# Two hybrid decoder layers on one core: the sparse indexer's heads paced by the projections instead of issued in bursts

## The chip, the cores and the metric

One core of a Trainium2 chip. The metric is the device time of one execution in microseconds (us). The kernel before takes 1270.34 us, the median of three runs (1268.72 to 1270.92). The engines are named as in the profile: PE multiplies matrices (PEld loads its weights), DVE, ACT and POOL do elementwise work, SP issues the transfers.

## The reference, cut to what matters

`x` is 512 tokens of 1024 features. It is normalized once, then goes through two layers of this form (rotary embedding is `rope`; layer 0 and layer 1 differ in weights alone):

```python
def hybrid_layer(x, p_i, positions, w_in, sinks, idx_k_g, idx_k_b, w_o, ...):
    qa, ka, va, qb, kb, vb, qi, ki, wi = split(x @ w_in)
    qi = rope(qi.reshape(B, S, IDX_HEADS, IDX_DIM), positions)
    ki = rope(layer_norm(ki, idx_k_g, idx_k_b), positions)
    wi = wi * (IDX_HEADS ** -0.5 * IDX_DIM ** -0.5)
    oa = swa_sink_attention(rope(qa), rope(ka), va, sinks)
    # inside dsa_sparse_attention, for each block of 128 queries:
    #   sc = einsum('bqhd,bsd->bqhs', qi, ki)
    #   idx_score = einsum('bqhs,bqh->bqs', relu(sc), wi), causal
    #   sel = the 128 best keys of each query; softmax attention over those
    ob = dsa_sparse_attention(rope(qb), rope(kb), vb, qi, ki, wi, k_top)
    x = layer_norm(DN_ALPHA * x + concat(oa, ob) @ w_o, ln1_g, ln1_b)
    g, u = split(x @ w_gu)
    ple = (p_i @ w_pp) * sigmoid(x @ w_pg)
    return layer_norm(DN_ALPHA * x + (silu(g) * u) @ w_down + ple, ln2_g, ln2_b)
```

There are 8 index heads of 32 features. The key `ki` of a token is shared by the heads and has a layer norm of its own with the gain `idx_k_g`.

## The kernel before, in words

The 512 tokens are four blocks t = 0 to 3 of 128. Every float32 product is made of three passes over a high and a low part (`mm3`, L317, L318, L319), so most of PE's instructions come from those three lines. `fh` and `fl` are the two parts of the residual stream with features in the partitions. `to_features` makes them: PE transposes (L430) a block into two PSUM banks, ACT copies the high part (L432), DVE subtracts for the low part (L433). PSUM has 8 banks in one rotation, all under the name `bank`.

**The front of a layer** is `start()`. For each block it projects the 296 index columns (256 of the queries, 32 of the key, 8 of the head weights), with `gi_out` behind the product. Then come the 384 key and value columns for two pairs of blocks (`kv_out`) and two of the four query projections of 256 columns (`q_out`). `gi_out` takes mean and variance of the index key from PSUM (L559, L560), copies the key into the tile `kin` (L558), and rotates the queries (`rope`: DVE L507, POOL L509, a rounded high part L512, the low part L513). For every second block it finishes the key's norm for two blocks: a reciprocal root in ten small DVE instructions (L349 to L356), then subtract the mean and multiply by the gain (L575), then multiply by the root and add (L576).

**Held turns.** What `gi_out` leaves must be transposed by PE (`turn`: PE L519, ACT L520). PE would have to wait for DVE and POOL if this came at once, so `order.later(delay, fn)` holds it: `Order` adds up an estimate of PE's time, and the held function runs when the sum has grown by `delay`. The index turns are held by D_GI = 9, the key turns by D_K = 8, the query turns by D_Q = 10.

**The index stream** is `index()`. For t = 1, 2, 3 it waits until the turns of its block are there. Then it writes one matmul for each of 8 heads over the keys up to its block (L650, 256, 384 or 512 columns), with ACT's relu behind it (L652) and DVE's weighted sum into `work` (L653). `topk()` follows on DVE: 16 steps of L664 and L665 for a block, then a mask (L667) which the sparse attention's scores read (L693).

**The order of the streams** is made by `Order.run`. Each stream is a generator with a clock of its own; the one furthest behind goes next, and what it yields is added to its clock. A stream that yields None waits, and its clock stands still. So `index()`, which has waited through the projections, has the lowest clock by far when its turns are there, and its heads come one after another until it has caught up. A scheduler behind this places each engine's instructions, and waits are added where one engine needs another.

**Before the first layer** the input norm of block 0 runs on DVE; blocks 1 to 3 take their sums on ACT (`ln_in_sums`: L374 the sum, L369 the squares), DVE applies them in `ln_in` (L389, L392). The rotary tables (`rotary`) are made on POOL and ACT beside that. `nsink`, the negated sinks, is one DVE instruction (L496). Weights arrive by SP, ACT rounds their high part (L270), POOL subtracts for the low part (L271).

## Time and profile before

| | |
|---|---|
| median of three runs | 1270.34 us (1268.72 to 1270.92) |
| the profiled execution | 1271.32 us, of it 1269.3 us span |
| mean granted clock of PE | 0.991 |
| PE busy | 1238.0 us, 98% of the span |
| DVE busy | 802.1 us, 63% |
| POOL busy | 702.3 us, 55% |
| ACT busy | 575.4 us, 45% |
| chain that ended last | PE 89%, DVE 4%, ACT 3%, POOL 2%, DMA 1% |

The span runs from the first to the last instruction; the profiled execution's own time has 2.0 us more around it. The clock is given in parts of 2.4 GHz: 1.00 is that level, 0.50 is 1.2 GHz. The chain is followed back from the last instruction: at each step to what released it. Its engine shares say whose work the end hung on. In the timelines the figure in brackets is idle time of the engine just before the row, with what ended it.

### The profile page before, as it was taken

The numbers are of one execution on the slowest core, as the hardware profiler recorded it, in microseconds if no ns is written. First come the engines' busy times: TensorE is split into PE (matmuls) and PEld (weight loads), VectorE is DVE, ScalarE is ACT, GpSimd is POOL, SyncE is SP. The second block draws the span as 40 slices with busy tenths as digits, with TensorE's granted clock in tenths as the row PEclk, the third lists the DMA queues.
The fourth block names the chain that finished last, engine by engine and source line by source line (L and its number), as shares of the span: only waits on it lengthen the run. The fifth ranks groups of instructions, "written<-read, shape, count | busy, mean of one in ns | idle before, by whom it ended". The sixth has DMA issues, their size and how long they took to land.

```text
span 1269.3 us, 18252 instructions
## 1 busy us (share of the span) xinstructions
PE 1238.0 (98%) x6632; PEld 1071.2 (84%) x6632; DVE 802.1 (63%) x1729; ACT 575.4 (45%) x1193; POOL 702.3 (55%) x579
## 2 busy tenths in 40 slices
PE   7899999999999999999999999999999999999996
PEld 5899989888888888888898998988888888888885
DVE  7889866764646363635679996675736364545376
ACT  6467764343333333434336677633434243433320
POOL 6687532367475756563067855233757574747422
PEclk9899999999999999999998999999999999999998
DMA  5133211333242424034023313114232323221321
GB/s 174 51 100 101 81 53 35 100 117 116 67 133 68 131 78 126 29 114 139 2 81 98 106 39 120 43 35 142 88 120 79 121 83 116 89 94 48 103 83 50
DMA packets 89123, 112.77 MB, mean 89 GB/s; under 512 B 5445, under 2 KB 65861, under 8 KB 89033
## 3 DMA queue, kind: packets, MB, share of 16 engines
q1 hardware_dynamic: 88360, 111.58, 28.2%
q8 instruction: 52, 0.85, 0.3%
q14 instruction: 39, 0.31, 0.1%
q10 hardware_dynamic: 672, 0.03, 0.0%
HBM read 109.49 MB, written 2.10 MB: 88 GB/s over the span
## 4 chain that ended last, share of the span: by engine, by line
PE 89%; DVE 4%; ACT 3%; POOL 2%; DMA 1%; issue 1%; DVEq 0%; ACTq 0%; SPq 0%; POOLq 0%
PE bank L317 26%; PE bank L318 26%; PE bank L319 26%; PE bank L689 3%; PE bank L731 2%; PE bank L725 2%; PE bank L519 1%; DMA wst<-in_w_pg_dram 1%; POOL wsp L271 1%; PE bank L430 1%; ACT wsp L270 1%; PE bank L748 1%; DVE x L413 1%; ACT bank L652 0%; DVE x L415 0%
## 5 line engine op out<-in xcount | busy, mean ns | idle before, releaser
L271 POOL TENSOR_TENSOR wsp<-wst,wsp 128x1024 fp32r<-128x1024 f32 (+2 forms) x148 | 351.5, 2388 | 270.9 <-ACT wsp L270 270.3
L318 PE MATMUL bank<-fl,wsp 128*128 128x512 f32 (+1 forms) x768 | 284.9, 372 | 0.4 <-DVE fl L433 0.4
L317 PE MATMUL bank<-fh,wsp 128*128 128x512 f32 (+1 forms) x768 | 283.6, 372 | 1.0 <-ACT fh L432 1.0
L319 PE MATMUL bank<-fh,wsp 128*128 128x512 f32 (+1 forms) x768 | 283.2, 371 | 0.0
L270 ACT CAST wsp<-wst 128x1024 fp32r<-128x1024 f32 (+2 forms) x148 | 151.4, 1032 | 166.4 <-PE bank L319 123.0
L881 DVE TENSOR_TENSOR t2k<-bank,t2k 128x512 f32<-128x512 f32 x44 | 30.4, 692 | 221.7 <-PE bank L319 221.7
L317 PE MATMUL bank<-wsp,fh 128*128 128x256 f32 (+3 forms) x512 | 166.9, 328 | 2.8 <-ACT fh L432 2.1
L319 PE MATMUL bank<-wsp,fl 128*128 128x256 f32 (+3 forms) x512 | 165.0, 325 | 1.8 <-DVE fl L433 1.1
L318 PEld LDWEIGHTS bank<-fl,wsp 128*128 128x128 f32 x768 | 144.7, 188 | 25.7 <-DVE fl L433 0.9
L317 PEld LDWEIGHTS bank<-fh,wsp 128*128 128x128 f32 x768 | 143.6, 188 | 26.7 <-ACT fh L432 1.9
L319 PEld LDWEIGHTS bank<-fh,wsp 128*128 128x128 f32 x768 | 144.7, 188 | 24.8
L318 PE MATMUL bank<-wsp,fh 128*128 128x256 f32 (+3 forms) x512 | 165.5, 324 | 0.0
L249 POOL TENSOR_TENSOR wsp<-slot,wsp 128x512 fp32r<-128x512 f32 x100 | 142.2, 1447 | 28.9 <-ACT wsp L248 28.9
L317 PE MATMUL bank<-wsp,slot 128*128 128x512 f32 x392 | 153.4, 391 | 0.0
L318 PE MATMUL bank<-wsp,slot 128*128 128x512 f32 x392 | 152.6, 389 | 0.0
L319 PE MATMUL bank<-wsp,slot 128*128 128x512 f32 x392 | 148.7, 390 | 0.0
L806 DVE TENSOR_TENSOR x<-bank,x 128x512 f32<-128x512 f32 x140 | 91.5, 684 | 88.5 <-PE bank L319 88.5
L911 ACT CAST slot<-t2k 128x256 fp32r<-128x256 f32 (+1 forms) x104 | 49.8, 497 | 144.0 <-DVE t2k L881 102.5
L249 POOL TENSOR_TENSOR wsp<-t2k,wsp 128x512 fp32r<-128x512 f32 x40 | 57.6, 1450 | 91.8 <-ACT wsp L248 91.8
L317 PEld LDWEIGHTS bank<-wsp,fh 128*128 128x128 f32 x512 | 98.7, 193 | 10.0 <-ACT fh L432 3.2
L319 PEld LDWEIGHTS bank<-wsp,fl 128*128 128x128 f32 x512 | 98.3, 193 | 7.7 <-DVE fl L433 1.6
L318 PEld LDWEIGHTS bank<-wsp,fh 128*128 128x128 f32 x512 | 98.9, 193 | 5.4
(169 smaller groups left out, 2174.0 us busy)
## 6 DMA issues: line engine op xcount, KB each, us to landing
wst<-in_w_gu_dram SPq DMA_DIRECT2D x88, 512.0 KB, 3.5
slot<-in_w_down_dram SPq DMA_DIRECT2D x80, 256.0 KB, 2.8
wst<-in_w_in_dram SPq DMA_DIRECT2D x16, 512.0 KB, 3.6
wst<-in_w_o_dram SPq DMA_DIRECT2D x16, 512.0 KB, 3.7
wst<-in_w_pg_dram SPq DMA_DIRECT2D x16, 512.0 KB, 4.1
wst<-in_w_in_dram SPq DMA_DIRECT2D x8, 256.0 KB, 2.8
lng<-in_ln_g_dram SPq DMA_DIRECT2D x4, 512.0 KB, 4.8
lnb<-in_ln_b_dram SPq DMA_DIRECT2D x4, 512.0 KB, 5.6
```

The costliest lines, as they stand in the source:

```text
L249: G.tensor_tensor(w[:, 1, j], src[j], w[:, 0, j], OP.subtract)
L270: A.copy(w[:, 0, :a * n], st[:, :a * n])
L271: G.tensor_tensor(w[:, 1, :a * n], st[:, :a * n], w[:, 0, :a * n], OP.subtract)
L317: PE.matmul(o, sh, mh, start=start, stop=False, skip_group_check=again)
L318: PE.matmul(o, sh, ml, start=False, stop=False, skip_group_check=again)
L319: PE.matmul(o, sl, mh, start=False, stop=stop, skip_group_check=again)
L689: PE.matmul(ps[:, o:o + nn], qT[kind, t, g][:, j * 128:(j + 1) * 128], kT[c, s][:, k0:k0 + nn], start=(s == 0), stop=(s == 1))
L725: PE.matmul(o, vt[b0 + b][:, f:f + 128], pts[b][:, u], start=b == 0 and u == 0, stop=b == nb - 1 and u == 1)
L731: PE.transpose(ps[:, j * 128:(j + 1) * 128], es[j][:, b * 128:(b + 1) * 128], idf)
L806: V.tensor_tensor(xt[t][:, c], ps, xt[t][:, c], OP.add)
L881: V.tensor_tensor(a, ps[1, f], a, OP.mult)
L911: A.copy(h[0], src)
```

## The change

Five edits, in the order of the diff.

1. `run` takes `credit=False`, used for `start()` with `index()`: a stream that waited begins again at the highest clock of the streams that did not wait. The index heads then come in turn with the projections.
2. The turns of the last block (t = 3, with the key of blocks 2 and 3) are held by D_KI = 13 instead of D_GI = 9. For blocks 0 to 2 the delay stays.
3. The copy into `kin` (L558) is gone. The subtraction of the mean and product with the gain stands right behind the block's mean and variance, and reads PSUM.
4. The sums of blocks 2 and 3 and the second half of the rotary tables are written inside `start()`, behind block 0's `to_features`; the sums of block 2 may not be placed ahead of ACT's second copy of the high part.
5. `nsink` is written at block 2, behind the last norm's DVE instruction.

```diff
--- before.py
+++ after.py
@@ -34,7 +34,7 @@
 THETA = 10000.0
 QA, KA, QB, KB, QI, NIN = 0, 512, 768, 1280, 1408, 1704
 NSLOT, NTMP = 28, 12
-D_GI, D_K, D_Q, AHEAD = 9.0, 8.0, 10.0, 2
+D_GI, D_KI, D_K, D_Q, AHEAD = 9.0, 13.0, 8.0, 10.0, 2
 IDX_PACE, NSTART, R_MAIN, R_TOP = 1.5, 2, 0.75, 0.001
 LAG, FILL = dict(a=1, b=2), {2: 6, 5: -2}
 QS = [("a", 0), ("a", 1), ("b", 0), ("b", 1)]
@@ -64,9 +64,12 @@
         while self.held:
             self.held.pop(0)[1]()
 
-    def run(self, *streams):
+    def run(self, *streams, credit=True):
+
+
 
         live = [[0.0, n, g, r] for n, (g, r) in enumerate(streams)]
+        waited = set()
         while live:
             live.sort(key=lambda e: e[:2])
             for e in live:
@@ -75,8 +78,13 @@
                 except StopIteration:
                     live.remove(e)
                     break
-                if c is not None:
+                if c is None:
+                    waited.add(e[1])
+                else:
                     c, pace = c if isinstance(c, tuple) else (c, c)
+                    if e[1] in waited and not credit:
+                        e[0] = max([e[0]] + [o[0] for o in live if o[1] not in waited])
+                    waited.discard(e[1])
                     e[0] += pace / e[3]
                     self.tick(c)
                     break
@@ -429,7 +437,7 @@
                 k = 4 * j + i
                 PE.transpose(ps[:, i * 128:(i + 1) * 128], xt[t][:, k * 128:(k + 1) * 128], idf)
             pv = ps.rearrange("p (a n) -> p a n", a=4)
-            A.copy(fh[:, 4 * j:4 * j + 4, ts], pv)
+            last["copy"] = A.copy(fh[:, 4 * j:4 * j + 4, ts], pv).ins
             V.tensor_tensor(fl[:, 4 * j:4 * j + 4, ts], pv, fh[:, 4 * j:4 * j + 4, ts], OP.subtract)
 
 
@@ -486,14 +494,10 @@
     ln_in(0)
     table = rotary()
     next(table)
-    for t in range(1, NT):
-        ln_in_sums(t)
-    for _ in table:
-        pass
+    ln_in_sums(1)
     bcast_row(ikg.rearrange("p a b -> p (a b)"), idx_k_g, 0, L * ID)
     bcast_row(ikb.rearrange("p a b -> p (a b)"), idx_k_b, 0, L * ID)
     bcast_row(sink.rearrange("p a b -> p (a b)"), attn_sinks, 0, L * NH)
-    V.tensor_scalar(nsink, sink, -1.0, None, op0=OP.mult)
 
     def rope(src, t, n, d, hi, lo, dup, each=False, top=None):
 
@@ -555,9 +559,10 @@
                 kin[t] = sm(2 * ID, "kin").rearrange("p (u d) -> p u d", u=2)
                 kmv[t] = sm(4, "kmv").rearrange("p (u d) -> p u d", u=2)
             st = sm(6, "kst6")
-            V.tensor_copy(kin[t - u][:, u], ps[:, 256:288])
             V.bn_stats(st, ps[:, 256:288])
             V.bn_aggr(kmv[t - u][:, u], st)
+            V.scalar_tensor_tensor(kin[t - u][:, u], ps[:, 256:288], kmv[t - u][:, u, 0:1], ikg[:, l],
+                                   op0=OP.subtract, op1=OP.mult)
             qs = []
             if t > 0:
                 wi[t] = small.tile([128, IH], F32, name="wi", tag="wi", bufs=4)
@@ -572,7 +577,6 @@
                 kn, mv = kin[t0], kmv[t0]
                 rs = rstd_of(mv[:, :, 1], 2)
                 for i in range(2):
-                    V.scalar_tensor_tensor(kn[:, i], kn[:, i], mv[:, i, 0:1], ikg[:, l], op0=OP.subtract, op1=OP.mult)
                     V.scalar_tensor_tensor(kn[:, i], kn[:, i], rs[:, i:i + 1], ikb[:, l], op0=OP.mult, op1=OP.add)
                 ks = slot()
                 iv = ks[:, :256].rearrange("p (t s u d) -> p t s u d", t=2, s=2, u=2)
@@ -587,7 +591,7 @@
                     turn(qiT[t, j], q, 4)
                 ready.add(("i", t))
                 order.tick(0.6)
-            order.later(D_GI, turns)
+            order.later(D_GI if t < NT - 1 else D_KI, turns)
 
         def kv_out(t, ps):
 
@@ -825,11 +829,20 @@
                 if l == 0 or t == 3:
                     to_features(t)
                     yield 0.9
+                if l == 0 and t == 0:
+                    with tc.issue_after(last["copy"]):
+                        ln_in_sums(2)
+                    ln_in_sums(3)
+                    for _ in table:
+                        pass
                 if l == 0 and t + 1 < NT:
                     ln_in(t + 1)
                 done = gi_out
                 if l == 0 and t + 1 < NT:
                     done = behind(last["norm"], gi_out)
+                if l == 0 and t == 2:
+                    with tc.issue_after(last["norm"]):
+                        V.tensor_scalar(nsink, sink, -1.0, None, op0=OP.mult)
                 yield from project(ws, 296, (t,), from_f, done, 3 * (t == 3))
             ws = take(4)
             for b in ALL:
@@ -847,7 +860,7 @@
                 for b in ALL:
                     yield from project(ws, 512, b, from_ma, res_out(h, ALPHA), 2 * (b is ALL[-1]))
 
-        order.run((start(), 1.0), (index(), 1.0))
+        order.run((start(), 1.0), (index(), 1.0), credit=False)
         load_gb(("1", l), ln1_g, ln1_b, l * D)
         order.run((rest(), R_MAIN), (attention(), 1.0), (topk(), R_TOP))
         order.flush()
```

Line numbers move by 4 to 8: `mm3` is L325, L326, L327, the turns L523, the index heads L654, L656, L657, POOL's weight parts L279, the low part of a rotation L517.

**PE, layer 0, at the index stream.** Before, all heads of t = 1, all turns of t = 2 and 3 and all heads of t = 2 stand between two groups of the 384-column projection (`x8`: eight in a row):

```order
L319 MATMUL bank<-wsp,fl 128x384
L650 MATMUL bank<-slot 128x256 x8
L519 MATMUL bank<-idr,slot 128x128 x18
L650 MATMUL bank<-slot 128x384 x8
L317 MATMUL bank<-wsp,fh 128x384
L318 MATMUL bank<-wsp,fh 128x384
```

With the change two heads of t = 1 stand there, then the turns of t = 2, then three heads, and the projection goes on:

```order
L327 MATMUL bank<-wsp,fl 128x384
L654 MATMUL bank<-slot 128x256 x2
L523 MATMUL bank<-idr,slot 128x128 x8
L654 MATMUL bank<-slot 128x256 x3
L325 MATMUL bank<-wsp,fh 128x384
L326 MATMUL bank<-wsp,fh 128x384
```

The other three heads of t = 1 come one at a time, 22 or more matmuls later, and the turns of t = 3 among them:

```order
L654 MATMUL bank<-slot 128x256
L325 MATMUL bank<-wsp,fh 128x384
L326 MATMUL bank<-wsp,fh 128x384
L327 MATMUL bank<-wsp,fl 128x384
L523 MATMUL bank<-idr,slot 128x128 x10
L325 MATMUL bank<-wsp,fh 128x384
L326 MATMUL bank<-wsp,fh 128x384
L327 MATMUL bank<-wsp,fl 128x384
L654 MATMUL bank<-slot 128x256
```

All the work of the burst is still there; 48 of the 384-column matmuls stand between the first head and the first 256-column matmul in both, but now they stand among the heads, and all but two of t = 2's heads and all of t = 3's come after the 256-column matmuls have begun.

**POOL, layer 0, while the turns' inputs are made.** `L512` and `L513` write the high and the low part of the rotated index queries, `L271` the low part of weights. Before, from the rotation of block 2 on:

```order
L509 TENSOR_TENSOR t2k<-t2k 128x4x32 x2
L512 CAST slot<-t2k 128x8x32
L271 TENSOR_TENSOR wsp<-wst,wsp 128x768
L512 CAST slot<-t2k 128x8x32
L271 TENSOR_TENSOR wsp<-wst,wsp 128x768
L513 TENSOR_TENSOR slot<-t2k,slot 128x8x32
L509 TENSOR_TENSOR t2k<-t2k 128x4x32 x2
L271 TENSOR_TENSOR wsp<-wst,wsp 128x1024
L513 TENSOR_TENSOR slot<-t2k,slot 128x8x32
```

With the change:

```order
L513 TENSOR_TENSOR t2k<-t2k 128x4x32 x2
L279 TENSOR_TENSOR wsp<-wst,wsp 128x768
L516 CAST slot<-t2k 128x8x32 x2
L279 TENSOR_TENSOR wsp<-wst,wsp 128x768
L279 TENSOR_TENSOR wsp<-wst,wsp 128x1024
L513 TENSOR_TENSOR t2k<-t2k 128x4x32 x2
L517 TENSOR_TENSOR slot<-t2k,slot 128x8x32 x2
```

The first low part (L513, now L517) came between the second and the third weight part and now comes behind the third; up to the second low part the set of instructions is the same.

**DVE, at the start.** `L389`/`L392` (now L397/L400) are the input norm, `fl` is the low part of block 0. Before:

```order
L392 SCALAR_TENSOR_TENSOR x_85<-x_85,lns_165,bank 128x512 x2
L389 SCALAR_TENSOR_TENSOR x_86<-x_86,lnm,bank 128x512 x2
L349 TENSOR_SCALAR lnv_274<-lnvar 128x1
L496 TENSOR_SCALAR nsink<-sink 128x16
L350 TENSOR_SCALAR lns_275<-lnv_274 128x1
L433 TENSOR_TENSOR fl<-bank,fh 128x4x128
L355 TENSOR_SCALAR lnt_276<-lns_275,lnv_274 128x1
L433 TENSOR_TENSOR fl<-bank,fh 128x4x128
```

With the change:

```order
L400 SCALAR_TENSOR_TENSOR x_85<-x_85,lns_165,bank 128x512 x2
L397 SCALAR_TENSOR_TENSOR x_86<-x_86,lnm,bank 128x512 x2
L357 TENSOR_SCALAR lnv_273<-lnvar 128x1
L441 TENSOR_TENSOR fl<-bank,fh 128x4x128 x2
L358 TENSOR_SCALAR lns_274<-lnv_273 128x1
```

`nsink` is gone from in front of `fl`, and both low parts come right behind L357.

## Rows read from the trace of the kernel before

**Rows 1.** the page's part 1: busy us, share of the span, instructions
```profile
PE 1238.0 (98%) x6632; PEld 1071.2 (84%) x6632; DVE 802.1 (63%) x1729; ACT 575.4 (45%) x1193; POOL 702.3 (55%) x579
```

**Rows 2.** PE's list of waits: us in total, times, longest us
```profile
PE bank L650 <- DVE work L653: 4.8, 5, 2.0
```

**Rows 3.** timeline of PE, layer 0: start us, us, instruction, [idle before <-releaser]
```profile
47.18 0.87 PE L650 MATMUL bank<-slot 128*128 128x256 f32 x6
...
49.75 0.39 PE L650 MATMUL bank<-slot 128*128 128x256 f32 x1 [1.70 <-DVE work L653]
...
52.55 1.51 PE L519 MATMUL bank<-idr,slot 128*128 128x128 f32 x10 [0.22 <-POOL slot L513]
...
57.63 0.69 PE L650 MATMUL bank<-slot 128*128 128x384 f32 x1 [0.76 <-DVE work L653]
...
61.14 0.34 PE L317 MATMUL bank<-wsp,fh 128*128 128x384 f32 x1
...
61.31 0.34 PE L318 MATMUL bank<-wsp,fh 128*128 128x384 f32 x1
...
70.66 0.38 PE L317 MATMUL bank<-wsp,fh 128*128 128x256 f32 x1 [0.41 <-ACT slot L618]
```

**Rows 4.** stretches: us, busy of PE, PEld, DVE, ACT, POOL, granted clock, DMA share, GB/s
```profile
47.18:61.14 13.96, 10.70 (x45) 8.84 (x45) 12.83 (x35) 10.11 (x31) 9.56 (x21) 0.63 0.14 40
...
667.60:678.96 11.36, 8.55 (x41) 7.14 (x39) 10.23 (x31) 8.71 (x27) 8.03 (x17) 0.70 0.28 83
...
51.00:52.00 1.00, 0.98 (x8) 0.97 (x8) 0.90 (x2) 0.35 (x2) 1.00 (x2) 0.50 0.01 3
...
840.00:860.00 20.00, 17.90 (x108) 15.46 (x106) 19.22 (x43) 9.55 (x14) 11.07 (x4) 1.00 0.26 80
```

**Rows 5.** timeline of PE, layer 1
```profile
667.62 0.87 PE L650 MATMUL bank<-slot 128*128 128x256 f32 x6
...
670.45 0.39 PE L650 MATMUL bank<-slot 128*128 128x256 f32 x1 [1.96 <-DVE work L653]
...
689.06 0.39 PE L317 MATMUL bank<-wsp,fh 128*128 128x256 f32 x1 [0.29 <-ACT slot L618]
```

**Rows 6.** timeline of DVE, layer 0, the index key and the first score
```profile
41.09 0.19 DVE L558 COPY kin<-bank 128x32 f32<-128x32 f32 x1 [1.30 <-PE bank L319]
...
42.23 1.85 DVE L349 TENSOR_SCALAR lnv<-kmv 128x2 f32<-128x2 f32 x1
...
49.22 0.47 DVE L653 SCALAR_TENSOR_TENSOR work<-bank,wi,causal 128x256 f32<-128x256 f32 x1
```

**Rows 7.** timeline of POOL beside it
```profile
42.20 1.85 POOL L271 TENSOR_TENSOR wsp<-wst,wsp 128x768 fp32r<-128x768 f32 x1
...
47.88 0.72 POOL L513 TENSOR_TENSOR slot<-t2k,slot 128x256 fp32r<-128x256 f32 x1
```

**Rows 8.** timeline of PE at the start
```profile
15.49 0.62 PE L317 MATMUL bank<-wsp,fh 128*128 128x296 f32 x1 [1.34 <-ACT fh L432]
...
17.45 0.62 PE L319 MATMUL bank<-wsp,fl 128*128 128x296 f32 x1 [1.10 <-DVE fl L433]
```

**Rows 9.** timeline of ACT at the start
```profile
13.84 1.04 ACT L374 ACTIVATE t2k<-x 128x1024 bf16<-128x1024 f32 x1
...
14.87 1.05 ACT L432 CAST fh<-bank 128x512 fp32r<-128x512 f32 x2
```

**Rows 10.** timeline of DVE at the start
```profile
15.28 0.15 DVE L349 TENSOR_SCALAR lnv<-lnvar 128x1 f32<-128x1 f32 x1
...
15.35 1.40 DVE L496 TENSOR_SCALAR nsink<-sink 128x16 f32<-128x16 f32 x1
...
16.72 0.68 DVE L433 TENSOR_TENSOR fl<-bank,fh 128x512 fp32r<-128x512 f32 x1
```

**Rows 11.** timeline of DVE, last block: top-k's mask and its first reader
```profile
150.99 0.42 DVE L667 TENSOR_SCALAR work<-work 128x512 f32<-128x512 f32 x1
...
186.65 0.68 DVE L693 CUSTOM_DVE_ANT_0 t2k<-bank,work 128x512 f32<-128x512 f32 x1
```

## The prediction

> **What bounds the kernel now.** I read the page's busy shares first. PE is busy 1238.0 us of a span of 1269.3 us [rows 1], so some 31 us of idle PE are all that an edit of order can win, and what PE does at half its clock comes on top. Next I read PE's list of waits to find those idle stretches. Its longest entry is the index heads: 4.8 us in five waits, the longest 2.0 us, each for DVE's weighted sum to free a PSUM bank [rows 2]. The timeline of PE shows the place. In layer 0 six heads of t = 1 are written from 47.18 us in 0.87 us. The seventh waits 1.70 us for a bank, the turns follow, then the heads of t = 2, and the projection of 384 columns is back only after 57.63 us [rows 3]. Layer 1 has the same figure from 667.62 us, with a wait of 1.96 us [rows 5].
>
> The stretches show a second loss. In 47.18 to 61.14 us the mean granted clock is 0.63, in layer 1's stretch 0.70, and from 51 to 52 us it is 0.50, the level of 1.2 GHz [rows 4]. It fell after PE had been mostly idle from about 48 to 50 us, and the step between two 384-column matmuls is back at 0.17 us only at 61.14 [rows 3]. A sparse PE is not always slowed: 840 to 860 us has 2.1 us of idle and a clock of 1.00 throughout [rows 4]. So the burst costs waits first and then low-clock work, the turns among it.
>
> **What the burst costs, in layer 0.** I price PE's work at the full clock. A 384-column matmul or head takes 0.17 us (61.14 to 61.31), a 256-column head 0.87 / 6 = 0.145, a turn's transpose half of 1.51 / 10, so 0.075, since that row ran at the low level [rows 3, 4]. A 512-column head scales to 0.17 x 512 / 384 = 0.23. From the first head at 47.18 to the first 256-column matmul at 70.66 are 23.5 us [rows 3]. Counted in the order of PE, this holds 8 small heads (1.2), 8 of 384 columns (1.4), 5 of 512 (1.1), 30 transposes (2.2) and 48 matmuls (8.2): 14.1 us. So **9.4 us are lost**.
>
> With the change the same way holds 8 small heads, 2 of 384 columns, 30 transposes and 48 matmuls: 11.9 us, and 2.2 us of heads come later. Two waits stay.
> - The first four transposes of t = 2 are reached at 47.5. They need low parts from POOL, and the first of these now stands behind a third weight part. The set of instructions up to the second low part is unchanged, so that ends at 47.88 + 0.72 = 48.6 [rows 7]. Then the third of the next three heads needs the bank of the first head, which DVE frees at 49.22 + 0.47 = 49.7 [rows 6]. The projection goes on at 49.8, where the work alone would be done at 48.5: 1.3 us lost.
> - At the key turns and the first 256-column matmuls PE needs banks from ACT's copies and DVE's first sums of t = 2. No row shows this wait. It is bounded by 0.41, the wait now at that place [rows 3], and by 2.0, the longest of the heads' waits [rows 2]. I take 2.0, since DVE has both jobs there.
>
> So 3.3 of 9.4 us stay: **6.1 us won**, 7.7 with the short second wait.
>
> **Layer 1.** From 667.62 to 689.06 are 21.4 us [rows 5]. The order holds 13.9 us there (4 heads of 512 columns instead of 5), so 7.6 are lost. With the change one head, 8 transposes and three heads take 1.2 us, to 668.8, and then the bank is waited for until 670.45, where DVE's first sum released it before [rows 5]: 1.65. With 2.0 for the second wait 3.9 us are won, 5.5 with 0.4.
>
> **The start.** ACT's copies of block 0's high part began at 14.87, behind the sums of block 2, which began at 13.84 [rows 9]. They change places: 1.0 us. DVE's low part began at 16.72, because `nsink` took from 15.35 to 16.75 [rows 10]; now it comes behind L349, at 15.4: 1.3 us. PE's first matmuls were held until 15.49 by the first and stopped again until 17.45 by the second [rows 8]. What follows is paced by PE, so I take **1.2 us**. The sums of block 2 come 1.05 us later on ACT [rows 9]; if block 2's norm became late by that, 0.3 would be left. `nsink` moves to block 2 and may hold DVE there for up to 1.4 us [rows 10], ahead of a wait PE does not have.
>
> **Edits at nothing.** Eight copies of 0.19 us leave DVE [rows 6]. The subtraction of the mean moves ahead of the root and out of the last chain of a pair; DVE's work there is beside PE's projection. If that cover went, the copies alone would be 8 x 0.19 = 1.5 us in my favour. The transfers on SP keep their order. The later heads make the top-k steps later: the last block's mask is done at 151.4 and first read at 186.65 [rows 11], 35 us of cover; without it the sparse scores of the last block wait.
>
> **Two allowances.** The spread stretch has places where PE still waits and the clock could fall. I take one fall in the two layers, at the price of the dense work that ran at the low level at the end of the old burst, 57.63 to 61.14: half of 3.5 us, 1.75 [rows 3]. The ends are 0 and the low level for all of it, which is a rival below. The 20 to 25 heads of a layer that now come late can each meet a full DVE queue; nothing shows it, between 0 and another 2.0 a layer [rows 2]. I take 1.0 for both layers, nearer to 0, since the five heads of 512 columns already stand among matmuls and cause none of the waits listed.
>
> A row bears on the second bound. DVE's L349, on two elements, took 1.85 us from 42.23, ending with POOL's weight part that ran from 42.20 to 44.05 [rows 6, 7]; on one element it took 0.15 [rows 10]. The weight parts now come closer together while the root of the index key is made, so one more such hold, 1.7 us a layer, is inside the bounds above. The Trainium skill's GPSIMD Engine Reference, section Specifications, says that GpSimd shares its SBUF interfaces with VectorE and names the kinds of DVE instructions that contend; the trace agrees with 1.85 against 0.15. By that rule with a hold in each layer, the sum would be 3.4 us smaller.
>
> **The sum.** 1.2 + 6.1 + 3.9 - 1.7 - 1.0 = 8.5 us. Against the profiled execution of 1271.3 us that is 1262.8. The median of the runs is 1.0 lower, so I forecast **1261.8 us**.
>
> **Rivals.**
> - *The clock falls again.* The sparse 47.5 to 49.8 lowers it as before, and it stays low as long as it did: a mean of 0.63 over 13.96 us, made of 1.00 and 0.50, is 10.3 us at the low level, and 0.70 over 11.36 us is 6.8 [rows 4]. At half speed these lose 5.1 us of now dense work in layer 0 and 3.4 in layer 1. Of 11.2 - 1.0 us won, 8.5 go: 1.7 stay, 1268.6 us. For it: the same waits on POOL and DVE open the stretch. Against: the idle piece is 1.3 us where it was over 2, the matmuls behind it are dense, and 840 to 860 us kept 1.00. I give 0.18. The Trainium skill has a rule that speaks for this rival: TensorE: Matmul & The Clock Gate, section HAM oscillation, tells of a kernel whose short bursts of matmuls between waits each start at the low clock. The trace agrees for 51 to 52 us (0.50) and not for 840 to 860 (1.00).
> - *Top-k becomes late: slower.* DVE is a queue in order, and the index sums of t = 2 and 3 now stand among the projections up to the sliding scores. If the last mask slips by more than 35 us [rows 11], the sparse scores of t = 3 start later than before whatever was won ahead of them. With a slip of 40 us they start at 191.4 instead of 186.65: 4.8 us in each layer, 1279.9 us. Against: in the changed order 42 of the 48 steps stand ahead of the first reader of even the first mask, and each mask ahead of its reader. 0.06.
> - *The change does not reach PE.* The heads are spread in the program, but ACT's relus stand in its queue behind casts that wait for POOL, and PE waits at each head for a bank as long in sum as it did. Then 9.4 and 7.6 us stay lost and the start alone is won: 1269.1 us, or no change. Against: PE's own order has the turns and 48 matmuls between the heads, and these do not need DVE's sums. 0.06.
>
> **How the numbers follow.** The forecast has 0.70. Its bounds: 1.4 + 7.7 + 5.5 with no allowances would be 14.6 us, 1255.7; I end the range at 1257, since all bounds at their best is unlikely, and at 1269.0, which takes in the first rival. Outside are the slower rival, most of the third and about 0.06 below. A measurement of this kernel can tell about 0.2%, 2.5 us, from no change. Faster by more: 0.70 and somewhat over half of the first rival, 0.80. The same: the rest of it and the third, 0.14. Slower: 0.06.
>
> **What would show it.** Right: PE's waits on the weighted sums under 2 us, a granted clock of 0.9 or more in 47 to 62 and 667 to 680 us, the first 256-column matmul near 61.2 and 675.9 (62.4 and 683.2 less what was won before them), PE's first low-part matmul near 16.1, and from there to the end the same durations. Wrong: a stretch at 0.50 among the 384-column matmuls, a new wait of some us at the key turns, a wait of the sparse scores on L671 (the mask), or a first block that starts no earlier.

## The result, and the profile after

The changed kernel takes 1262.15 us, the median of four runs (1261.93 to 1264.07), beside 1270.63 for the kernel before in the same comparison. The ratio is 0.9938 with a 95% interval of 0.9921 to 0.9955: **8.5 us faster**, where 8.5 had been forecast. The two profiled executions differ by somewhat more, 1271.32 against 1261.93, and their spans by 9.3 us (1269.3 and 1260.0). The sums below go by the spans, so they hold 0.8 us that the medians do not show.

The page's busy shares of the changed kernel answer to [rows 1]:

```profile
PE 1230.5 (98%) x6632; PEld 1064.6 (84%) x6632; DVE 796.7 (63%) x1721; ACT 575.1 (46%) x1193; POOL 700.3 (56%) x579
```

PE is busy 7.5 us less, with the same 6632 matmuls: a matmul at the lower clock counts as busy for longer (a row of 384 columns takes 0.52 us in the old burst and 0.33 in the new stretch), and that work is gone. Next PE's list of waits (us in total, times, the longest), which answers to [rows 2]:

```profile
PE bank L752 <- POOL rb L709: 2.5, 2, 1.5
...
PE bank L325 <- DVE work L657: 2.2, 2, 1.2
...
PE bank L327 <- DVE fl L441: 0.8, 1, 0.8
...
PE bank L523 <- POOL slot L517: 0.5, 2, 0.3
...
PE bank L654 <- DVE work L657: 0.3, 1, 0.3
```

The 4.8 us in which heads waited for a bank are 0.3 now. The projection waits 2.2 us for the same sums in two places. On top of the list of new waits stands one that the prediction does not name: 2.5 us for `rb`, the reciprocals of the softmax, which POOL copies (L709). PE's timeline shows the places in layer 0, to be read beside [rows 3]:

```profile
45.45 0.40 PE L654 MATMUL bank<-slot 128*128 128x256 f32 x2
...
46.15 0.54 PE L523 MATMUL bank<-idr,slot 128*128 128x128 f32 x4 [0.30 <-POOL slot L517]
...
46.84 0.54 PE L523 MATMUL bank<-idr,slot 128*128 128x128 f32 x4 [0.15 <-POOL slot L517]
...
47.21 0.59 PE L654 MATMUL bank<-slot 128*128 128x256 f32 x3
...
53.26 0.97 PE L523 MATMUL bank<-idr,slot 128*128 128x128 f32 x10
...
57.60 1.14 PE L620 MATMUL bank<-idr,slot 128*128 128x128 f32 x12
...
59.98 0.38 PE L325 MATMUL bank<-wsp,fh 128*128 128x256 f32 x1 [1.23 <-DVE work L657]
...
164.68 0.44 PE L752 MATMUL bank<-idf,rb 128*128 128x128 f32 x2 [1.00 <-POOL rb L709]
```

In 45.45 to 59.98 there are three idle pieces: 0.30, 0.15 and 1.23 us. The ten transposes at 53.26 take 0.97 us where they took 1.51. The stretches from the first head to the first 256-column matmul of each layer answer to [rows 4] (us, busy of PE, PEld, DVE, ACT, POOL, granted clock, DMA share, GB/s):

```profile
45.45:59.98 14.53, 12.84 (x90) 12.29 (x89) 7.18 (x21) 11.10 (x33) 13.93 (x24) 1.00 0.25 64
...
659.90:674.50 14.60, 12.98 (x89) 12.43 (x89) 7.54 (x21) 10.81 (x34) 14.36 (x25) 1.00 0.32 93
...
59.00:60.00 1.00, 0.03 (x1) 0.03 (x1) 1.00 (x3) 1.00 (x7) 1.00 (x2) 1.00 0.94 319
```

The clock is 1.00 in both, and it stays there through the one microsecond with 0.03 us of PE (59 to 60). At the start the shift is there too, beside [rows 8] and [rows 10]:

```profile
14.44 0.61 PE L325 MATMUL bank<-wsp,fh 128*128 128x296 f32 x1 [0.25 <-ACT fh L440]
...
16.08 0.61 PE L327 MATMUL bank<-wsp,fl 128*128 128x296 f32 x1 [0.77 <-DVE fl L441]
```

```profile
15.34 1.28 DVE L441 TENSOR_TENSOR fl<-bank,fh 128x512 fp32r<-128x512 f32 x2
```

Reading the same marks in both traces gives the account of the 9.3 us. A mark's time is the start of its first instruction; a lead is what the change is ahead there.

| mark | before | after | lead |
|---|---|---|---|
| first low-part matmul | 17.45 | 16.08 | 1.4 |
| layer 0, first head | 47.18 | 45.45 | 1.7 |
| layer 0, first 256-column matmul | 70.66 | 59.98 | 10.7, of it 2.2 put off |
| layer 0, first transpose of the norm after the output projection | 228.33 | 220.94 | 7.4 |
| layer 1, first head | 667.62 | 659.90 | 7.7 |
| layer 1, first 256-column matmul | 689.06 | 674.50 | 14.6, of it 1.9 put off |
| layer 1, first transpose of that norm | 846.30 | 836.81 | 9.5 |
| span | 1269.3 | 1260.0 | 9.3 |

"Put off" is the work of heads that stood ahead of the mark before and stands behind it now, priced as in the prediction. So the start won 1.7, the index stages 6.8 and 4.9, and between the index stage and the norm 1.1 us were lost in layer 0 and 3.1 in layer 1. That last loss is where the surprise lies. The figure for layer 0 leans on one trace: the kernel before takes 23.5 us there, and 22.1 in the run of it with the copy on ACT further down, whose instructions are the same in that stretch. Against that one 5.4 us are won.

### The profile page after: what moved, and what is told of

Its sections match the earlier page's. It is cut to its first block, busy times and chain, and to the rows that moved or that the text cites. A ratio compares the mean times of both kernels' runs of the same rounds, so it can differ in the third digit from the quotient of the medians.

```text
span 1260.0 us, 18247 instructions
## 1 busy us (share of the span) xinstructions
PE 1230.5 (98%) x6632; PEld 1064.6 (84%) x6632; DVE 796.7 (63%) x1721; ACT 575.1 (46%) x1193; POOL 700.3 (56%) x579
## 3 DMA queue, kind: packets, MB, share of 16 engines
q1 hardware_dynamic: 88360, 111.58, 28.7%
## 4 chain that ended last, share of the span: by engine, by line
PE 91%; DVE 3%; POOL 2%; ACT 2%; issue 1%; DMA 1%; SPq 0%; DVEq 0%; POOLq 0%; ACTq 0%
PE bank L325 27%; PE bank L326 27%; PE bank L327 27%; PE bank L693 2%; PE bank L735 2%; PE bank L729 2%; POOL wsp L279 1%; PE bank L523 1%; DMA wst<-in_w_in_dram 1%; PE bank L438 1%; PE bank L752 1%; POOL slot L517 1%; DVE x L421 1%; PE bank L654 1%; ACT wsp L278 0%
## 5 line engine op out<-in xcount | busy, mean ns | idle before, releaser
L279 POOL TENSOR_TENSOR wsp<-wst,wsp 128x1024 fp32r<-128x1024 f32 (+2 forms) x148 | 351.2, 2387 | 271.4 <-ACT wsp L278 269.2
L326 PE MATMUL bank<-fl,wsp 128*128 128x512 f32 (+1 forms) x768 | 284.9, 372 | 0.4 <-DVE fl L441 0.4
L325 PE MATMUL bank<-fh,wsp 128*128 128x512 f32 (+1 forms) x768 | 283.6, 372 | 1.0 <-ACT fh L440 1.0
L327 PE MATMUL bank<-fh,wsp 128*128 128x512 f32 (+1 forms) x768 | 283.2, 371 | 0.0
L325 PE MATMUL bank<-wsp,fh 128*128 128x256 f32 (+3 forms) x512 | 164.7, 326 | 3.8 <-DVE work L657 2.2
L325 PEld LDWEIGHTS bank<-fh,wsp 128*128 128x128 f32 x768 | 143.6, 188 | 26.8 <-ACT fh L440 1.9
L326 PEld LDWEIGHTS bank<-fl,wsp 128*128 128x128 f32 x768 | 144.7, 188 | 25.6 <-DVE fl L441 0.9
L327 PEld LDWEIGHTS bank<-fh,wsp 128*128 128x128 f32 x768 | 144.7, 188 | 25.0
L327 PE MATMUL bank<-wsp,fl 128*128 128x256 f32 (+3 forms) x512 | 163.2, 321 | 1.3 <-DVE fl L441 0.8
L326 PE MATMUL bank<-wsp,fh 128*128 128x256 f32 (+3 forms) x512 | 164.1, 321 | 0.0
L325 PE MATMUL bank<-wsp,slot 128*128 128x512 f32 x392 | 153.4, 391 | 0.0
L326 PE MATMUL bank<-wsp,slot 128*128 128x512 f32 x392 | 152.8, 390 | 0.0
L327 PE MATMUL bank<-wsp,slot 128*128 128x512 f32 x392 | 148.7, 390 | 0.0
L325 PEld LDWEIGHTS bank<-wsp,fh 128*128 128x128 f32 x512 | 97.0, 191 | 10.4 <-ACT fh L440 2.9
L327 PEld LDWEIGHTS bank<-wsp,fl 128*128 128x128 f32 x512 | 97.3, 191 | 7.1 <-DVE fl L441 1.1
L326 PEld LDWEIGHTS bank<-wsp,fh 128*128 128x128 f32 x512 | 97.7, 191 | 5.5
```

The lines of the kernel that those rows point to most:

```text
L279: G.tensor_tensor(w[:, 1, :a * n], st[:, :a * n], w[:, 0, :a * n], OP.subtract)
L325: PE.matmul(o, sh, mh, start=start, stop=False, skip_group_check=again)
L326: PE.matmul(o, sh, ml, start=False, stop=False, skip_group_check=again)
L327: PE.matmul(o, sl, mh, start=False, stop=stop, skip_group_check=again)
```

## The experiments

Twelve kernels ran, each timed in five rounds against the kernel before. Theory and rival stand with each as they were written ahead of the run.

**One edit undone: the credit.** The index stream keeps its credit, the turns of t = 3 are still held by 13.

```diff
-        order.run((start(), 1.0), (index(), 1.0), credit=False)
+        order.run((start(), 1.0), (index(), 1.0))
```

> The change without its first edit: the index stream keeps its credit, so eight heads of t = 1 stand in a row, but the turns of t = 3 are still held by 13. Theory (the burst of heads costs the waits and the clock): the wait of about 1.7 us for a bank stays in each layer and the clock may still fall behind it, so about half of what the index stage gave is lost: 1266 to 1267 us. Rival (the turns of t = 3 in the burst were the cost, and holding them by 13 is the whole remedy): 1262 to 1263 us, the clock near 1.00 from 47 to 62 us.

Measured: 1277.22 us, ratio 1.0052 (1.0039 to 1.0064). Both sides missed: it is slower than the kernel before. PE in layer 0:

```profile
47.35 0.38 PE L654 MATMUL bank<-slot 128*128 128x256 f32 x1 [0.38 <-DVE work L657]
...
59.05 1.21 PE L654 MATMUL bank<-slot 128*128 128x384 f32 x6
...
62.40 0.44 PE L654 MATMUL bank<-slot 128*128 128x384 f32 x1 [2.15 <-DVE work L657]
...
64.17 2.57 PE L654 MATMUL bank<-slot 128*128 128x512 f32 x3 [0.16 <-DVE work L657]
```

```profile
64.00:72.00 8.00, 6.80 (x26) 4.74 (x26) 8.00 (x22) 6.44 (x25) 4.54 (x8) 0.50 0.48 136
```

The eight heads of t = 1 stand alone now, and the projection does go on behind them. But `index()` waits 31 more matmuls for the turns of t = 3, its clock stands still, the last 17 of the 384-column matmuls go by as well, and then all eight heads of t = 2 and three of t = 3 come in a row. These are longer, DVE is busy throughout (8.00 of 8.00 us from 64 to 72), and PE's granted clock is 0.50 over those 8 us. So the delay of the turns is no remedy by itself: it moves the burst and makes it larger.

**One edit undone: the delay.** The turns of t = 3 are held by 9 again.

```diff
-            order.later(D_GI if t < NT - 1 else D_KI, turns)
+            order.later(D_GI, turns)
```

> The change without its second edit: the turns of t = 3 are held by 9 again and stand among the heads of t = 1, ahead of the projection. Theory (heads are the cost): most of the gain stays, 1263 to 1264.5 us, with one more wait of PE for a low part from POOL of about 1 us in each layer. Rival (turns of t = 3 are the cost): the waits for POOL's low parts and the low clock come back, 1267 to 1269 us.

Measured: 1265.73 us, ratio 0.9964 (0.9952 to 0.9977), by the ratios 3.3 us behind the change and between the two ranges. The mechanism is the rival's, the size is half of it:

```profile
50.35 1.51 PE L523 MATMUL bank<-idr,slot 128*128 128x128 f32 x10 [2.55 <-POOL slot L517]
...
666.86 1.05 PE L523 MATMUL bank<-idr,slot 128*128 128x128 f32 x10 [3.86 <-POOL slot L517]
```

```profile
48.00:50.00 2.00, 0.00 (x0) 0.00 (x0) 0.97 (x2) 0.66 (x3) 2.00 (x5) 1.00 0.00 0
...
50.00:54.00 4.00, 3.65 (x19) 3.65 (x20) 0.91 (x3) 2.43 (x8) 1.79 (x5) 0.57 0.01 4
```

The turns of t = 3 are reached while POOL still writes their low part. PE waits 2.55 and 3.86 us, does nothing at all from 48 to 50, and the clock is 0.57 over the next four microseconds. Without a credit this is paid once in each layer, not for a burst.

**The start.** The fourth and fifth edits undone, and then the two alone in the kernel before (both are the hunks of the diff at L494 and L829).

> The change without its fourth and fifth edits (sums, tables and the negated sinks where they were). Theory: PE's first low-part matmul is again near 17.4 us and everything behind is 1.4 to 1.7 us later: 1263.6 to 1264.0 us. Rival (the shift at the start is absorbed by the index stage's own wait on DVE and POOL): no more than 0.5 us later, 1262.2 to 1262.7.

> The kernel before with the fourth and fifth edits alone. Theory: PE's first low-part matmul near 16.1 us and the whole program 1.2 to 1.7 us earlier, 1268.7 to 1269.3 us. Rival (absorbed by the burst's waits, which hang on DVE and POOL and not on PE): within 0.5 us of the kernel before.

Measured: 1263.71 us without them (ratio 0.9945, 0.9932 to 0.9959), 1268.75 with them alone (0.9991, 0.9982 to 0.9999). Alone they give 0.0009 of 1270, so 1.1 us, and PE's first low-part matmul is at 16.14, as expected. Undone, the median is 1.6 us behind the change (0.9 by the ratios), in the theory's range, but the intervals overlap. In its trace the first low-part matmul comes at 18.70 and the first head at 47.78, 2.6 and 2.3 us later than with the change. Of that, 1.2 us are not the edits' doing: the input arrived later in this execution. DVE's first instruction on it, here and then in the changed kernel:

```profile
7.58 1.40 DVE L372 BATCH_NORM_STATS2 bst<-x 128x6 f32<-128x512 f32 x2 [5.62 <-DMA x<-in_x_dram]
```

```profile
6.35 1.40 DVE L372 BATCH_NORM_STATS2 bst<-x 128x6 f32<-128x512 f32 x2 [4.40 <-DMA x<-in_x_dram]
```

Without these 1.2 the shift is 1.4 us at the low part and 1.1 at the first head. It is there and is not absorbed, and its size is about 1 to 1.4 us.

**The key's chain.** The third edit undone.

```diff
+            V.tensor_copy(kin[t - u][:, u], ps[:, 256:288])
             V.bn_stats(st, ps[:, 256:288])
             V.bn_aggr(kmv[t - u][:, u], st)
-            V.scalar_tensor_tensor(kin[t - u][:, u], ps[:, 256:288], kmv[t - u][:, u, 0:1], ikg[:, l],
-                                   op0=OP.subtract, op1=OP.mult)
...
                 for i in range(2):
+                    V.scalar_tensor_tensor(kn[:, i], kn[:, i], mv[:, i, 0:1], ikg[:, l], op0=OP.subtract, op1=OP.mult)
                     V.scalar_tensor_tensor(kn[:, i], kn[:, i], rs[:, i:i + 1], ikb[:, l], op0=OP.mult, op1=OP.add)
```

> The change without its third edit: the copy of the index key and the later subtraction are back. Theory (hidden beside PE's projections): within 0.7 us of the change, 1261.5 to 1263.0 us. Rival (the key's chain on DVE sets the first index sum, for which PE waits in both layers): that sum comes about 1 us later in each layer, 1263.5 to 1265 us.

Measured: 1263.17 us, ratio 0.9951 (0.9938 to 0.9963), between the two ranges; the interval overlaps the change's, so the time alone decides nothing. The trace speaks for the rival at half its size. DVE in layer 0, the first instruction of the chain and the first index sum, without the edit and then with it:

```profile
39.36 0.19 DVE L562 COPY kin<-bank 128x32 f32<-128x32 f32 x1 [1.30 <-PE bank L327]
...
47.49 0.47 DVE L657 SCALAR_TENSOR_TENSOR work<-bank,wi,causal 128x256 f32<-128x256 f32 x1
```

```profile
38.82 0.20 DVE L562 BATCH_NORM_STATS2 kst<-bank 128x6 f32<-128x32 f32 x1 [1.57 <-PE bank L327]
...
46.17 0.48 DVE L657 SCALAR_TENSOR_TENSOR work<-bank,wi,causal 128x256 f32<-128x256 f32 x1 [0.33 <-ACT bank L656]
```

The chain takes 8.1 us without the edit, as before (41.09 to 49.22 [rows 6]), and 7.4 with it, of which 0.3 is a wait for ACT. It also begins 0.5 us later without the edit (39.36 against 38.82), although PE's first low-part matmul is at 16.08 in both; why is not known. PE's waits show the later sums: in layer 0 for the low parts 0.94 instead of 0.45, in layer 1 for the first sum 1.48 instead of 1.02.

```profile
46.92 0.54 PE L523 MATMUL bank<-idr,slot 128*128 128x128 f32 x4 [0.94 <-POOL slot L517]
...
663.28 0.44 PE L325 MATMUL bank<-wsp,fh 128*128 128x384 f32 x1 [1.48 <-DVE work L657]
```

**The pace of the heads.** 1.0 and 2.2 instead of 1.5.

```diff
-IDX_PACE, NSTART, R_MAIN, R_TOP = 1.5, 2, 0.75, 0.001
+IDX_PACE, NSTART, R_MAIN, R_TOP = 1.0, 2, 0.75, 0.001
```

> The change with the index heads' pace at 1.0 instead of 1.5, so five heads of t = 1 stand behind the first turns and all heads come earlier. Theory (the late top-k on DVE makes the new waits for rb, 2.5 us in all, and earlier heads take them away; but more heads in a row wait for banks): waits for rb under 1 us, waits on the index sums 1 to 2 us longer in each layer, together 1261.5 to 1264 us. Rival (only the spread counts, the less spread the worse): 1265 to 1268 us with the waits for rb still there.

Measured: 1260.43 us, ratio 0.9930 (0.9918 to 0.9943). The list of waits has 0.6 us for `rb` instead of 2.5, and 2.5 for the index sums, about what it was (2.8). So the theory's first half holds and the added bank waits did not come; the time is a little better than its range, and its interval overlaps the change's.

> The change with the pace at 2.2: the heads are spread further and the top-k of t = 3 begins later. Theory (top-k has little cover left): the last mask comes later and PE waits for rb or for the masked scores for 2 to 8 us in each layer, 1266 to 1278 us. Rival (the cover is still large, more spread is harmless): 1260 to 1263 us.

Measured: 1268.26 us, ratio 0.9992 (0.9983 to 1.0001). The time lies in the theory's range, its mechanism is only in part there. The last mask of layer 0 comes 3.2 us later than with the change (159.75 against 156.56), the wait for `rb` is 1.00 us in layer 0 as with the change, and no wait stands at the masked scores. Part of the cost is another burst: the projections of `start()` run out before the heads do, and in layer 0 the eight heads of t = 3 stand in a row, with waits behind them.

```profile
85.75 2.08 PE L654 MATMUL bank<-slot 128*128 128x512 f32 x8
...
88.78 0.38 PE L325 MATMUL bank<-wsp,fh 128*128 128x256 f32 x1 [0.95 <-DVE work L657]
...
98.52 0.50 PE L693 MATMUL bank<-slot 128*128 128x256 f32 x2 [1.54 <-ACT slot L524]
```

Another part is the clock. In layer 1 PE waits 1.35 us at the first 256-column matmul, and the mean granted clock behind that wait is 0.59 over 4.15 us:

```profile
677.85 0.39 PE L325 MATMUL bank<-wsp,fh 128*128 128x256 f32 x1 [1.35 <-DVE work L657]
```

```profile
677.85:682.00 4.15, 4.15 (x22) 4.15 (x23) 0.65 (x2) 3.40 (x14) 4.15 (x6) 0.59 0.81 234
```

PE is idle 2.1 us more than with the change between the first heads and the norms of the two layers, and the low clock there takes an estimated 1.7 us (4.15 x 0.41). The span is 6.1 us longer, so over 2 us of it are not located.

**The new wait.** The copy of the reciprocals goes from POOL to ACT.

```diff
-            G.tensor_copy(rb.rearrange("p (j d) -> p j d", j=4), sums[:, :, None].to_broadcast([128, 4, 64]))
+            A.copy(rb.rearrange("p (j d) -> p j d", j=4), sums[:, :, None].to_broadcast([128, 4, 64]))
```

> The change with the copy of the softmax's reciprocals (rb) on ACT instead of POOL. Theory (PE's new wait of 2.5 us for rb is POOL's queue, where the copy stands behind a weight part of 2.4 us): the wait is gone, 1259.7 to 1261 us. Rival (the wait hangs on DVE's reciprocal, late behind the top-k): the wait moves to ACT or stays, 1261.7 to 1263 us.

Measured: 1259.04 us, ratio 0.9921 (0.9908 to 0.9933). The median is better than the theory's range; the interval overlaps the change's, but the wait is gone from the list and the span is 3.0 us shorter (1257.0; by the ratios it is 2.2 us). From the first 256-column matmul to the norm the run is 1.0 us shorter in layer 0 and 2.2 in layer 1. Why the wait was there is read in the trace of the changed kernel, POOL's queue in layer 0 and layer 1, and DVE in layer 1:

```profile
161.90 2.38 POOL L279 TENSOR_TENSOR wsp<-wst,wsp 128x1024 fp32r<-128x1024 f32 x1 [0.97 <-ACT wsp L278]
...
164.24 0.39 POOL L709 COPY rb<-sums 128x256 f32<-128x256 f32 x1
...
777.81 2.38 POOL L279 TENSOR_TENSOR wsp<-wst,wsp 128x1024 fp32r<-128x1024 f32 x1 [0.98 <-ACT wsp L278]
...
780.13 0.40 POOL L709 COPY rb<-sums 128x256 f32<-128x256 f32 x1
```

```profile
771.76 2.44 DVE L671 TENSOR_SCALAR work<-work 128x512 f32<-128x512 f32 x1
...
777.36 0.17 DVE L707 RECIPROCAL sums<-sums 128x4 f32<-128x4 f32 x1
```

```profile
771.55 2.38 POOL L279 TENSOR_TENSOR wsp<-wst,wsp 128x1024 fp32r<-128x1024 f32 x1 [8.60 <-ACT wsp L278]
```

In both layers the copy stands behind a weight part of 2.38 us and starts the moment that is done. In layer 1 DVE had the reciprocals at 777.5, the copy starts at 780.13, and PE's transposes of `rb` at 780.58. In front of that stands a second delay: the last mask (L671) takes 2.44 us, until just behind the end of the weight part that POOL began at 771.55, where in layer 0 it took 0.43 and before 0.42 [rows 11]. With the copy on ACT that mask runs ahead of the weight part (0.43 us at 770.69), so in layer 1 both delays go, and the run does not price them apart. The Trainium skill's GPSIMD Engine Reference, section Specifications, says that GpSimd's SBUF interfaces are shared with VectorE; the trace agrees with 2.44 against 0.43, and the prediction had seen the same on L349 [rows 6].

The same edit in the kernel before asks whether the wait belongs to the change:

> The kernel before with the copy of the softmax's reciprocals (rb) on ACT. Theory (the wait for rb exists only where the index heads, and so the top-k, come late): nothing is gained, within 0.8 us of the kernel before. Rival (POOL's queue delays rb in either kernel): 2 to 3 us faster, as with the change.

Measured: 1271.22 us, ratio 1.0010 (1.0001 to 1.0019). Nothing is gained, and there is no wait for `rb` in its list. So the wait was made by the change. That the late top-k makes it, as the theory has it, is not shown: the wait does not grow with the lateness of the heads. It is 0.6 us in all at a pace of 1.0, 2.5 at 1.5 and 1.0 at 2.2, and 0.7 without the delay. What decides in which of these kernels a copy meets a weight part stays open.

**Better than both.** The copy on ACT with a pace of 1.0 and of 1.25.

> The change with rb on ACT and the index heads' pace at 1.0. Theory (both remove the same wait for rb, and the pace also adds bank waits in the index stage): not better than rb on ACT alone, 1258.5 to 1260.5 us. Rival (the two gains, 3.1 and 1.7 us, add): 1257 to 1258 us.

> The change with rb on ACT and the pace at 1.25. Theory: between the pace of 1.5 and 1.0 with rb on ACT, 1258 to 1260 us. Rival (gains add): 1257.5 to 1258.5 us.

Measured: 1259.93 us (0.9927, 0.9914 to 0.9939) and **1257.80 us** (0.9905, 0.9890 to 0.9920). The gains of pace 1.0 and of the copy do not add, as the theory said. Its reason is only half there: PE waits for `rb` again, now 1.2 us in two waits for ACT, and the waits on the index sums (2.3 us) are no longer than with the pace of 1.5. The pace of 1.25 lies a little under the theory's range and inside the rival's, and its interval overlaps that of 1.5 with the copy on ACT, so these two are not told apart; it is faster than the change by about 4 us and than the kernel before by about 12.

**What the clock costs.** In the kernel before, each head of t = 1 and 2 is written three times into its bank, with the same result. This keeps PE busy in the burst and does nothing else.

```diff
-                    PE.matmul(ps[:, :nk], qiT[t, h // 4][:, (h % 4) * 128:(h % 4 + 1) * 128], kiT[:, :nk],
-                              start=True, stop=True)
+                    for _ in range(3 if t < 3 else 1):
+                        PE.matmul(ps[:, :nk], qiT[t, h // 4][:, (h % 4) * 128:(h % 4 + 1) * 128], kiT[:, :nk],
+                                  start=True, stop=True)
```

> The kernel before with each index head of t = 1 and t = 2 written three times into its bank (same result, 32 more matmuls in each layer, 4.6 us of work at the full clock), in the same burst. Theory (the burst is bound by DVE's sums, and the clock that falls in it costs something of its own, about 1.75 us a layer): most of the added work fills waits that are there anyway; if the clock then stays near 1.00, the time is 0 to 3 us less than before in spite of more work, 1266 to 1270 us. Rival (the clock costs nothing, or the added work is not hidden): 1271 to 1279 us.

Measured: 1271.05 us, ratio 1.0007 (0.9998 to 1.0016), no change that can be told, and at the lower edge of the rival's range. The time allows two readings: the low clock cost nothing and the added work was hidden, or a gain from the clock went into added work that was not hidden. The stretches, as [rows 4], show that the clock did rise, from 0.63 to 0.88 and from 0.70 to 1.00:

```profile
47.18:61.14 13.96, 13.09 (x77) 12.23 (x76) 13.02 (x38) 10.48 (x31) 8.79 (x20) 0.88 0.13 39
...
667.60:679.00 11.40, 10.20 (x66) 9.07 (x66) 10.50 (x30) 8.75 (x27) 7.80 (x19) 1.00 0.17 49
```

The marks decide. The first 384-column matmul behind the burst, in the kernel before and then in this run, which also shows layer 0's first 256-column matmul:

```profile
58.12 0.66 PE L317 MATMUL bank<-wsp,fh 128*128 128x384 f32 x1
...
676.88 0.69 PE L317 MATMUL bank<-wsp,fh 128*128 128x384 f32 x1
```

```profile
58.42 0.33 PE L317 MATMUL bank<-wsp,fh 128*128 128x384 f32 x1
...
69.40 0.38 PE L317 MATMUL bank<-wsp,fh 128*128 128x256 f32 x1 [0.31 <-DVE work L654]
...
676.45 0.45 PE L317 MATMUL bank<-wsp,fh 128*128 128x384 f32 x1
```

The run of the kernel before with `rb` on ACT is a second witness. In layer 0 its burst has the instructions of the kernel before, without added work, and its clock came back earlier:

```profile
56.90 0.45 PE L317 MATMUL bank<-wsp,fh 128*128 128x384 f32 x1
...
68.11 0.39 PE L317 MATMUL bank<-wsp,fh 128*128 128x256 f32 x1 [0.41 <-ACT slot L618]
```

```profile
46.00:56.90 10.90, 7.11 (x36) 5.26 (x35) 9.80 (x25) 8.54 (x26) 7.73 (x18) 0.84 0.19 51
...
56.90:59.90 3.00, 3.00 (x17) 3.00 (x18) 3.00 (x11) 1.57 (x7) 1.80 (x4) 1.00 0.00 0
```

The table takes these marks from the first heads (47.18 and 667.62 before, 46.00 with `rb` on ACT, 46.37 and 666.49 in this run) to the first 256-column matmuls (70.66 and 689.06, 68.11, 69.40 and 687.98).

| stage | first head to the projection's return (mean clock) | from there to the first 256-column matmul |
|---|---|---|
| layer 0, before | 10.94 (0.67) | 12.54, its first 3.0 us at 0.50 |
| layer 0, before with `rb` on ACT | 10.90 (0.84) | 11.21 |
| layer 0, heads written three times | 12.05 (0.86) | 10.98 |
| layer 1, before | 9.26 (0.74) | 12.18, its first 2.1 us at 0.51 |
| layer 1, heads written three times | 9.96 (1.00) | 11.53 |

Inside the burst the lower clock cost nothing: 10.94 and 10.90 us at 0.67 and 0.84. Behind it the same projection took 1.3 us less where the clock was back, and 1.6 less in this run. In layer 1 its first six matmuls take 1.16 us where they took 2.08. The added work was hidden only in part: it makes the bursts 1.1 and 0.7 us longer, and in layer 1 two heads that stand behind the mark cost another 0.7. So gain and cost balance. The theory is right that the low clock has a price of its own, near its 1.75 in layer 0 and about half of that in layer 1, and too hopeful about the hiding; of the rival only the second half holds.

## Why the prediction was right, step by step

**The bound and the mechanism** held. The idle PE and the low clock at the index heads were the room, and both went. How the first two edits work together is shown by four runs. With neither, and the start moved, the ratio is 0.9991; with the credit gone alone 0.9964; with the delay alone 1.0052; with both 0.9938 (the last three have the third edit as well, the first has not). So taking the credit away wins about 3.4 us by itself, the third edit included, and 14.5 where the delay is there, and the delay wins 3.3 us where the credit is gone and loses over 7 where it is not. Each needs the other. Neither the prediction nor the first theory saw that the delay alone would do harm.

**The sum** is right to 0.1 us in the medians (0.8 short by the spans). That it is so close is luck: terms of both signs were off, each by 0.7 to 3.2 us but for the start. By the marks above:

| term of the sum | forecast | measured |
|---|---|---|
| start | 1.2 | 1.4 at the first low part, 1.7 at the first head |
| layer 0, index stage | 6.1 | 6.8 |
| layer 1, index stage | 3.9 | 4.9 |
| one fall of the clock | -1.7 | 0 |
| late heads | -1.0 | -4.2 |

- *Start.* The working holds. ACT's copies, DVE's low part and PE's matmul all moved as it says. In a run of its own the edit gave 1.1 us, with an interval of 0.1 to 2.3. The 0.3 us more at the first head are not shown to be the edit's: in the traces of the kernel before the way from the first low part to the first head takes 28.7 to 29.7 us.
- *Waits in the index stage.* In layer 0 the wait for the bank of the first head, part of a loss of 1.3, is not there. The first sum runs at 46.17 instead of 49.22, 3.0 us earlier, while PE's first head is only 1.7 earlier: the start and the shorter chain of the index key both reach it. What stays is 0.45 us for the low parts. The second wait is 1.23, between its bounds of 0.41 and 2.0. In layer 1 the waits are 1.02 and 0.61 against 1.65 and 2.0. Taking the upper end for a wait that no row shows was too careful. Two signs named in advance missed all the same: the waits on the weighted sums are 2.8 us in the whole kernel where under 2 was named, and the way behind the index stage did not keep its length. The hold on the key's root that the prediction prices at up to 3.4 us did not become more frequent: it comes once in each layer as before, 1.77 us on L358 and 1.25 on L357 where it was 1.85 and 1.56 on L349.
- *The clock.* In the stretches of the change it never fell. The price of a fall was right in size (1.3 to 1.6 us in layer 0 of the kernel before, against 1.75), but there was no fall to pay for. The rule of the Trainium skill that spoke for the first rival (TensorE: Matmul & The Clock Gate, section HAM oscillation) is seen in the run without the delay (0.57 behind a wait of 2.55 us) and in that with the pace of 2.2 (0.59 behind 1.35 us), not in the change (1.00 at 1.23 us).
- *Late heads: the term that was mis-sized.* The prediction allowed 1.0 us for heads that meet a full DVE queue. Heads wait 0.3 us in all, and yet 4.2 us went. By the list of waits 2.5 of them are the wait for `rb`; the run with the copy on ACT has a span shorter by 3.0, with the mask's delay in layer 1 among them. It is not the "top-k becomes late" rival: of the cover of 35 us some 21 are left in layer 0 (the last mask ends at 157.0 and is first read at 178.62), and the masked scores never waited. The prediction looked for this loss at the heads and their sums; it arose behind them, in POOL's queue. What makes the rest, about 1 us in layer 1, is not settled.
- *The edits at nothing.* For the index key this step failed, in a small way: the prediction put DVE's work there beside PE's projection, but the chain's end sets the first sum, for which PE waits. By the traces it is worth 0.8 us of span (1260.8 to 1260.0), within the 1.5 named for a lost cover; the times alone do not tell it from nothing. Whether the copies or the place of the subtraction did it was not tried.
- *"The change does not reach PE"* is out, and the slower rival did not decide, although spreading further (pace 2.2) does lose nearly all that was won.

## What to carry to other kernels

A stream that waits should not keep its claim: in a list scheduler like this one the credit grows with the wait and is spent as a burst on whatever engine is next, here DVE's sums and the PSUM banks. Try such edits together and apart: here one won some 3 us by itself, the other lost over 7, and together they won more than the first alone. After such an edit, look further on for new waits: here the largest was for a copy of 0.4 us in a queue behind weight parts of 2.4 us, worth 2 to 3 us, and it did not exist before the edit. A test that adds work to keep an engine busy must be read at marks along the trace, since its time mixes what the work costs with what it gives. And when a bound is priced by hand, a sum that comes out right may still be a sum of errors; the marks along the trace tell.

## What the runs showed of the hardware

- A DVE instruction from SBUF to SBUF can take until the end of a POOL tensor_tensor that runs beside it: the mask L671 took 2.44 us beside one of 2.38 and 0.43 without, in the same kernel, and 2.08 beside one with the pace of 2.2.
- What a low granted clock costs depends on what PE does meanwhile. In the burst of layer 0, where PE waits for DVE again and again, a mean of 0.67 or 0.84 made no difference (10.94 and 10.90 us); in the dense projection behind it the low level cost 1.3 us (12.54 and 11.21).
- The length of an idle piece of PE does not by itself tell whether the clock falls. It fell behind 2.55 us (0.57 over the four microseconds after 50, without the delay) and behind 1.35 us (0.59, pace of 2.2), and it stayed at 1.00 in the change behind 1.23 us (59.98) and 1.50 us (780.58).
